# A four-layer hybrid trunk on one core: finer write tracking, head outputs copied out of PSUM, and a new order table

## The chip, the cores and the metric

The kernel runs on one core of one Trainium2 chip. Its time is device microseconds of one execution; three executions of the kernel before gave 1045.62, 1047.05 and 1047.22 us, a median of 1047.05 us. A profiled execution of the same kernel took 1047.38 us. The engines are named as in the profile: PE (TensorE, matrix products and transposes), DVE (VectorE), ACT (ScalarE), POOL (GpSimd), SP (which issues the DMA transfers here). PE writes to PSUM, the small accumulator memory; everything else lives in SBUF.

## The reference

The input is x, 512 tokens of 1024 channels, in float32. Four layers follow, and each adds its output to x. Layers 0 and 3 are differential attention (A), layer 1 is a Conformer convolution (B), layer 2 is latent attention (C). Each also makes a SiLU gate that multiplies its branch before the output projection. Cut to what the change touches:

```python
# A: 8 heads, two softmax maps a head, blocks of 128 queries, chunk-causal
wts = p[:, :, 0] - lam * p[:, :, 1]
outs.append(jnp.einsum('bhqk,bhkd->bhqd', wts, v[:, :, :e]))
o = _rms_norm(jnp.concatenate(outs, axis=2), sub_g) * (1.0 - lambda_init)
return (o * jax.nn.silu(gate)) @ w_out

# B: GLU, causal depthwise convolution of 31 taps, LayerNorm, SiLU, gate
u = a * jax.nn.sigmoid(b)
u = lax.conv_general_dilated(u, conv_w, padding=[(B_CONV - 1, 0)], ...) + conv_b
u = jax.nn.silu(_layer_norm(u, ln_g, ln_b))
return (u * jax.nn.silu(gate)) @ w_out
```

## The kernel before

The 1024 channels are 8 blocks of 128, the 512 tokens 4 tiles of 128. Every float32 product is made of three fast ones: each operand is split into a high half (a rounded copy, mostly a cast on ACT, L497) and a low half (the difference, L514 on DVE or L517 on POOL), and PE computes high·high, high·low and low·high (L460). A projection runs through weight pieces of 128×1024 (tiles such as `L_g_w`, `L_o_w`), which SP loads, ACT casts, and DVE or POOL completes. `Hh` and `Hl` are the two halves of the normalised input; `X` is the residual stream.

**Attention (layers 0 and 3).** For head h and query block j, PE makes two score tiles (`L_h5j_sc`), DVE takes the maximum, ACT the exponentials (`_p`), DVE combines the maps; PE transposes them (`_wtr`, L466), ACT copies that to SBUF (`_wt`, L497), and PE multiplies with V into the head's output `L_o` (four query blocks of 128 columns, one PSUM buffer of the tag `o`, of which there is one slot). Four Square instructions on ACT (`_osq`) with sums, a root on POOL (`_or_y`, L740) and `gate_o` on DVE (L526: output times root times gate G, written to V) finish the head; only then is the slot `o` free for the next head's products. G comes from gate chunk 1: ACT scales it, loads the SiLU table, applies SiLU to 128×2048 elements, and loads the exponential's table again. The tiles `L_ytr` are transposes of V for the output projection.

**Convolution (layer 1).** `L_u` holds the GLU's result. The 8 channel blocks are convolved in three ways: some on DVE by 30 multiply-adds (`L_c`, L526), some on POOL from products of ACT (`L_cq` += `L_ct`, L517; the last addition writes `L_cs`), and blocks 5, 6 and 7 on PE (`conv_phase`): the rows are moved by DMA to `L_u4x` buffers (four groups of 32 partitions), DVE makes banded weights `L_wa` (four for a block, through the two buffers of the tag `p`), and PE multiplies, 72 matmul records a block. Blocks of the first two kinds come back to token order by transposes (`L_ctr`), blocks of the third land so. The result is V; BN_STATS on DVE takes statistics, and once all 8 blocks are there, an aggregate, a root on POOL (`L_lnr_y`) and 8 TENSOR_SCALAR instructions (L535) normalise V. Then V is transposed (`L_ytr`), ACT applies SiLU (`L_yv`), DVE multiplies by the gate and splits into `L_y`, and the output projection `L_o` runs. Gate chunk 1 (`L_g_a`, 96 matmuls of 512 columns) has no part in the LayerNorm.

**What sets the order.** The program makes a list of nodes (one instruction, or a group that stays together). `Plan.order` (L571) gives every engine its fixed sequence: of the nodes whose inputs and buffer slots are ready, by a cost model, the one that can start first goes next, ties by priority. The priority is the place in the program plus a number from the table `SHIFT`, looked up by layer, tile and engine. Each engine then runs its sequence strictly in order and waits by semaphores. What a node depends on comes from `Buf` and `View` (L79 to L195): every buffer keeps its last writer and its readers for each grain of elements and each half of the 128 partitions (`halves`).

## Time and profile before

| | |
|---|---|
| median of 3 runs | 1047.05 us (1045.62 to 1047.22) |
| profiled execution, its own time | 1047.38 us |
| its span, first to last instruction | 1045.6 us |
| mean granted PE clock | 0.990 |
| PE busy | 1006.7 us |
| DVE busy | 762.4 us |
| ACT busy | 585.1 us |
| POOL busy | 194.8 us |

The span is what the trace covers; the 1.8 us between it and the execution's time lie outside. Names in the rows lose their numbers: `L_o` is any head's output or any output projection of any layer, `L_ytr` any of the transposes of V. `[5.04 <-DVE V L535]` behind a row says that its engine was idle for 5.04 us before it, and that what it waited for last was DVE's write of V at line 535. A row with x8 groups eight instructions that ran one after another.

### The profile page before, as it was taken

How to read it: one execution, taken by the hardware profiler on the slowest of the kernel's cores; microseconds unless marked ns; L12 is line 12 of the kernel's file. 1: busy time of each engine (PE TensorE's matmuls, PEld its weight loads, DVE VectorE, ACT ScalarE, POOL GpSimd, SP SyncE). 2: the span in 40 equal slices, each digit the busy share in tenths (PEclk: the TensorE clock that was granted, in tenths of full speed). 3: DMA queues.
4: the chain of work that ended last, by engine and by line, in shares of the span. 5: the costliest groups of instructions: out<-in, count | busy, mean ns of one | idle time of the engine just before them, and what ended most of it. 6: DMA issues, size and time to landing. Idle time of an engine off the chain costs nothing.

```text
span 1045.6 us, 15204 instructions
## 1 busy us (share of the span) xinstructions
PE 1006.7 (96%) x5204; PEld 846.2 (81%) x5204; DVE 762.4 (73%) x1970; ACT 585.1 (56%) x1222; POOL 194.8 (19%) x135
## 2 busy tenths in 40 slices
...
GB/s 235 93 101 122 61 122 121 66 87 56 41 61 121 122 89 101 66 90 1 73 83 78 71 50 61 22 39 101 119 72 152 38 84 121 102 81 120 22 21 81
DMA packets 74308, 87.53 MB, mean 84 GB/s; under 512 B 17109, under 2 KB 47701, under 8 KB 74232
## 3 DMA queue, kind: packets, MB, share of 16 engines
...
## 4 chain that ended last, share of the span: by engine, by line
PE 72%; DVE 14%; ACT 6%; issue 4%; POOL 2%; DMA 1%; SPq 0%; DVEq 0%; ACTq 0%; POOLq 0%
PE L_o L460 20%; PE L_g_a L460 14%; PE L_qk_a L460 12%; PE L_v_a L460 8%; DVE L_c L526 4%; PE L_ab_a L460 2%; PE L_c_a L460 1%; POOL L_cq L517 1%; PE L_c L460 1%; DVE L_qk_T L514 1%; PE L_qk_tr L466 1%; ACT G L490 1%; PE L_kv_a L460 1%; DVE L_qk_t L514 1%; PE L_h3j_sc L460 1%
## 5 line engine op out<-in xcount | busy, mean ns | idle before, releaser
L460 PE MATMUL L_qk_a<-L_qk_w,Hh 128*128 128x512 f32 x512 | 161.6, 397 | 0.0
L460 PE MATMUL L_o<-L_y,L_o_w 128*128 128x512 f32 x576 | 141.6, 395 | 0.0
L460 PE MATMUL L_g_a<-L_g_w,Hh 128*128 128x512 f32 x384 | 121.4, 397 | 2.3 <-ACT L_qk_sq L490 1.9
L460 PEld LDWEIGHTS L_o<-L_y,L_o_w 128*128 128x128 f32 x576 | 105.2, 188 | 21.1 <-POOL L_o_w L517 0.4
L740 POOL TENSOR_TENSOR L_h_or_y<-L_h_ov,minus_half 128x4 f32<-128x4 f32 x16 | 17.4, 1089 | 484.3 <-DVE L_h_ov L535 311.7
L460 PEld LDWEIGHTS L_qk_a<-L_qk_w,Hh 128*128 128x128 f32 x512 | 92.5, 188 | 16.8 <-ACT G L490 0.3
L460 PE MATMUL L_qk_a<-L_qk_w,Hl 128*128 128x512 f32 x256 | 100.5, 392 | 0.6 <-DVE Hl L526 0.6
L517 POOL TENSOR_TENSOR L_cq<-L_cq,L_ct 128x512 f32<-128x512 f32 x58 | 80.2, 1382 | 27.9 <-DMA L_ab_w_r<-b_w_in 21.3
L460 PE MATMUL L_ab_a<-Hh,L_ab_w 128*128 128x512 f32 x256 | 81.6, 393 | 3.0 <-DVE L_ab_sg L514 2.1
L460 PEld LDWEIGHTS L_g_a<-L_g_w,Hh 128*128 128x128 f32 x384 | 69.6, 188 | 16.6 <-ACT L_qk_sq L490 2.3
L460 PE MATMUL L_v_a<-L_v_w,Hh 128*128 128x512 f32 x256 | 81.0, 397 | 0.7 <-DVE L_qk_t L514 0.5
L460 PE MATMUL L_g_a<-L_g_w,Hl 128*128 128x512 f32 x192 | 75.2, 391 | 0.0
L526 DVE SCALAR_TENSOR_TENSOR L_c<-L_u,L_tab,L_c 128x512 f32<-128x512 f32 x90 | 65.0, 750 | 1.4
L490 ACT ACTIVATE L_ct<-L_u,L_tab 128x512 f32<-128x512 f32 x60 | 42.6, 721 | 33.3 <-POOL L_cq L517 31.6
L460 PEld LDWEIGHTS L_ab_a<-Hh,L_ab_w 128*128 128x128 f32 x256 | 47.9, 188 | 15.4 <-DVE L_ab_sg L514 2.0
L460 PEld LDWEIGHTS L_qk_a<-L_qk_w,Hl 128*128 128x128 f32 x256 | 48.0, 188 | 11.9 <-DVE Hl L526 1.7
L460 PEld LDWEIGHTS L_v_a<-L_v_w,Hh 128*128 128x128 f32 x256 | 46.2, 188 | 9.9 <-DVE L_qk_t L514 1.0
L517 POOL TENSOR_TENSOR L_sqs<-L_sqs,L_sq 128x512 f32<-128x512 f32 x21 | 32.1, 1528 | 98.3 <-ACT L_sq L490 84.5
L514 DVE TENSOR_TENSOR L_g_w<-L_g_w_r,L_g_w 128x1024 fp32r<-128x1024 f32 x32 | 43.9, 1374 | 8.8 <-ACT L_g_w L497 8.2
L460 PE MATMUL L_v_a<-L_v_w,Hl 128*128 128x512 f32 x128 | 50.1, 391 | 0.0
L460 PE MATMUL L_ab_a<-Hl,L_ab_w 128*128 128x512 f32 x128 | 49.9, 390 | 0.0
L497 ACT CAST L_o_w<-L_o_w_r 128x1024 fp32r<-128x1024 f32 x32 | 33.6, 1052 | 28.7 <-PE L_g_a L460 16.4
...
## 6 DMA issues: line engine op xcount, KB each, us to landing
...
```

The lines of the kernel that those rows point to most:

```text
L460: lambda nc: nc.tensor.matmul(out.real(), a.real(), b.real(), start=start, stop=stop),
L466: emit = lambda nc: nc.tensor.transpose(out.real(), src.real(), ident.real())
L490: nc.scalar.activation(out.real(), src.real(), func, scale=scale.real() if isinstance(scale, View) else scale, **kw)
L497: lambda nc: nc.scalar.copy(out.real(), src.real()), [src], [out])
L514: lambda nc: nc.vector.tensor_tensor(out=out.real(), in0=a.real(), in1=b.real(), op=op), [a, b], [out])
L517: lambda nc: nc.gpsimd.tensor_tensor(out=out.real(), in0=a.real(), in1=b.real(), op=op), [a, b], [out])
L526: self.add("dve", out.n / 960.0 + (0.13 if isinstance(scalar, View) else 0.068), lambda nc: nc.vector.scalar_tensor_tensor(out=out.real(), ...
L740: self.p.add("pool", 0.32 + 0.18 * v.n, lambda nc: nc.gpsimd.tensor_tensor(out=y.real(), in0=v.real(), in1=self.minus_half[:, 0:v.n].real( ...
```

## The change

Three things change. Lines below the edits move by 3 (L460 becomes L463, L497 becomes L500, L517 becomes L520).

First, the tracking of writes. Buffers of 544 elements a partition (the `u4` buffers of `conv_phase`) are tracked in grains of 8 elements, those of 1084 (the GLU's `u`) in grains of 2, where both had 32; and partitions in four parts of 32, where there were two halves of 64. An instruction depends on fewer others by that where it touches only a part of such a buffer.

Second, in layers 0 and 3 the outputs of heads 4, 5 and 6 are copied from the PSUM slot `o` to an SBUF buffer `oc`, one query block at a time, by ACT. The squares and the gate multiply read the copy. These are 24 more ACT instructions.

Third, the whole `SHIFT` table is replaced by other numbers. The program has the same instructions otherwise.

```diff
-        self.grain = 1 if size <= 64 else 6 if size == 192 else 32
+        self.grain = 1 if size <= 64 else 6 if size == 192 else 8 if size == 544 else 2 if size == 1084 else 32
...
-        self.writer = [None] * (2 * n)
-        self.readers = [[] for _ in range(2 * n)]
+        self.writer = [None] * (4 * n)
+        self.readers = [[] for _ in range(4 * n)]
...
-            v.halves = tuple(range((rows.start or 0) // 64, -(-(rows.stop or P) // 64)))
+            v.parts = tuple(range((rows.start or 0) // 32, -(-(rows.stop or P) // 32)))
...
 SHIFT = {k: int(v) for k, v in (x.split("=") for x in """
-L0_g0_a.act=5733 L0_g0_a.pe=-1495 L0_g0_w.dve=1051 L0_g0_w_r.sp=-99 L0_g1_a.act=4 L0_g1_a.pe=1821 L0_g1_w.act=-392
...
-        return 0.115 if len(out.halves) == 1 and out.n > 256 else 0.0
+        return 0.115 if len(out.parts) <= 2 and out.n > 256 else 0.0
...
             sq = self.buf("mid", N + "_osq")
+            if 4 <= h < 7:
+                own = self.buf("mid", N + "_oc", [P, NT, P])
+                for jb in range(NT):
+                    p.copy(own[:, jb, :], po[:, jb, :])
+                po = own
             for jb in range(NT):
                 p.act(sq[:, jb * P:(jb + 1) * P], po[:, jb, :], AF.Square, accum=ss[:, jb:jb + 1])
```

What the new table does to the order is seen in the engines' sequences. PE at the end of layer B, before (`L_g_a` are gate matmuls, `L_c` with `L_wa` is block 7, `L_ctr` the transposes of blocks 2, 4, 3 and, last, 1, `L_ytr` those of V):

```order
L460 MATMUL L_g_a_4296<-Hl,L_g_w_4280 128x512
L460 MATMUL L_g_a_4296<-Hh,L_g_w_4280 128x512
L466 MATMUL L_ctr_4519<-ident,L_cs_4084 128x128 x4
L466 MATMUL L_ctr_4527<-ident,L_cs_4329 128x128 x4
L466 MATMUL L_ctr_4549<-ident,L_cs_4532 128x128 x4
L460 MATMUL L_c_4379<-L_wa_0_4371,L_u_4380 128x128 x9
L460 MATMUL L_c_4379<-L_wa_1_4382,L_u_4380 128x128 x9
L460 MATMUL L_c_4379<-L_wa_2_4583,L_u_4380 128x128 x9
L460 MATMUL L_c_4379<-L_wa_3_4595,L_u_4380 128x128 x9
L466 MATMUL L_ctr_4606<-ident,L_cs_4035 128x128 x4
L466 MATMUL L_ytr_4639<-ident,V 128x128 x4
```

and with the change, from block 7 on (`L_ctr_4512` is block 3):

```order
L463 MATMUL L_c_4330<-L_wa_0_4358,L_u_4331 128x128 x9
L463 MATMUL L_c_4330<-L_wa_1_4371,L_u_4331 128x128 x9
L463 MATMUL L_g_a_4480<-Hh,L_g_w_4191 128x512
L463 MATMUL L_g_a_4480<-Hl,L_g_w_4191 128x512
L463 MATMUL L_g_a_4480<-Hh,L_g_w_4191 128x512
L463 MATMUL L_c_4330<-L_wa_2_4473,L_u_4331 128x128 x9
L463 MATMUL L_c_4330<-L_wa_3_4484,L_u_4331 128x128 x9
L469 MATMUL L_ctr_4512<-ident,L_cs_4499 128x128 x4
L463 MATMUL L_g_a_4520<-Hh,L_g_w_4191 128x512
```

Block 7 has moved into the gate chunk, and block 3 behind it. The end of a run of gate matmuls and the first three transposes of V, further down in the same sequence:

```order
L463 MATMUL L_g_a_4520<-Hl,L_g_w_4258 128x512
L463 MATMUL L_g_a_4520<-Hh,L_g_w_4258 128x512
L469 MATMUL L_ytr_4592<-ident,V 128x128 x4
L469 MATMUL L_ytr_4598<-ident,V 128x128 x4
L469 MATMUL L_ytr_4606<-ident,V 128x128 x4
L463 MATMUL L_g_a_4440<-Hh,L_g_w_4258 128x512
L463 MATMUL L_g_a_4440<-Hl,L_g_w_4258 128x512
```

Before, all 96 gate matmuls stood ahead of the transposes and of block 7. Now 24 of them do; between the last `L_ctr` and the first `L_ytr` stand 39, and the rest lie among and behind the first transposes of V, ahead of the output projection.

POOL at the same place (`L_cq` and `L_cs` are block 3's sums, `L_o_w` low halves of output weights, `L_lnr_y` the LayerNorm's root), before:

```order
L517 TENSOR_TENSOR L_cq_3616<-L_cq_3616,L_ct_27_4386 128x512
L517 TENSOR_TENSOR L_o_w_4397<-L_o_w_r,L_o_w_4397 128x1024
L517 TENSOR_TENSOR L_cq_3616<-L_cq_3616,L_ct_28_4409 128x512
L517 TENSOR_TENSOR L_cq_3616<-L_cq_3616,L_ct_29_4417 128x512
L517 TENSOR_TENSOR L_o_w_4454<-L_o_w_r,L_o_w_4454 128x1024
L517 TENSOR_TENSOR L_o_w_4484<-L_o_w_r,L_o_w_4484 128x1024
L517 TENSOR_TENSOR L_cs_4532<-L_cq_3616,L_ct_30_4459 128x128x4
L517 TENSOR_TENSOR L_o_w_4524<-L_o_w_r,L_o_w_4524 128x1024
L740 TENSOR_TENSOR L_lnr_y<-L_v,minus_half 128x4
```

and now:

```order
L520 TENSOR_TENSOR L_cq_3615<-L_cq_3615,L_ct_28_4471 128x512
L520 TENSOR_TENSOR L_cq_3615<-L_cq_3615,L_ct_29_4478 128x512
L520 TENSOR_TENSOR L_cs_4499<-L_cq_3615,L_ct_30_4496 128x128x4
L743 TENSOR_TENSOR L_lnr_y<-L_v,minus_half 128x4
L520 TENSOR_TENSOR L_o_w_4556<-L_o_w_r,L_o_w_4556 128x1024
L520 TENSOR_TENSOR L_o_w_4581<-L_o_w_r,L_o_w_4581 128x1024
L520 TENSOR_TENSOR L_o_w_4648<-L_o_w_r,L_o_w_4648 128x1024
L520 TENSOR_TENSOR L_o_w_4695<-L_o_w_r,L_o_w_4695 128x1024
```

The four low halves of the first column half have moved from among and behind block 3's sums to directly behind the root.

ACT in the tail of layer 3, with the change, around the SiLU of gate chunk 1 (`L_h_oc` is the copy of head 5's or 6's output, `L_y` the next layer's or the projection's operand). Before, the two table loads and the SiLU stood ahead of head 5's last exponentials; now they stand around head 6's second weight copy:

```order
L493 ACTIVATE L_h_osq,L_h_oss<-L_h_oc 128x128
L493 ACTIVATE L_y_9448<-L_ytr_9597,L_lay 128x512
L493 ACT_TABLE_LOAD
L493 ACTIVATE G<-G 128x4x512
L500 COPY L_h6j_wt<-L_h6j_wtr 128x256
L493 ACT_TABLE_LOAD
L493 ACTIVATE L_h6j_p,L_l_9533<-L_h6j_sc_9580,L_h6j_mx_9605,L_rq 128x384
L493 ACTIVATE L_h6j_p,L_l_9533<-L_h6j_sc_9585,L_h6j_mx_9619,L_rq 128x384
```

Head 5 and 6 have by then written their first blocks into `o`, since the copies freed it.

More of the change, by code (lines that the diff above doesn't have):

```diff
@@ L117, with __init__ @@
 class View:
-    def __init__(self, buf, ops, idx, halves=(0, 1)):
-        self.buf, self.ops, self.idx, self.halves = buf, ops, idx, halves
+    def __init__(self, buf, ops, idx, parts=(0, 1, 2, 3)):
+        self.buf, self.ops, self.idx, self.parts = buf, ops, idx, parts
     def _then(self, op, idx):
-        return View(self.buf, self.ops + [op], idx, self.halves)
+        return View(self.buf, self.ops + [op], idx, self.parts)
     def __getitem__(self, i):
@@ L192, in grains @@
             u = np.unique(self.idx // self.buf.grain)
-            g = self._g = np.concatenate([u + h * self.buf.n for h in self.halves])
+            g = self._g = np.concatenate([u + h * self.buf.n for h in self.parts])
         return g
@@ new lines @@
+L0_h5_mx.dve=-461 L0_h5_oc.dve=2810 L0_h5_or_y.dve=6 L0_h5_osq.act=-2916 L0_h5_oss.dve=-928 L0_h5_ov.dve=1999
+L0_h5_p.dve=-1658 L0_h5_sc.dve=79 L0_h5_sc.pe=3337 L0_h5_wtr.pe=-4014 L0_h6_cf.dve=-15978 L0_h6_mx.dve=-323
+L0_h6_oc.act=14 L0_h6_or_y.pool=706 L0_h6_ov.dve=-2033 L0_h6_p.act=541 L0_h6_p.dve=-17 L0_h6_sc.dve=-787
+L0_h6_wt.act=-1587 L0_h7_cf.dve=-3972 L0_h7_or_y.dve=-2174 L0_h7_osq.act=313 L0_h7_oss.dve=762 L0_h7_p.act=2782
+L0_h7_p.dve=72 L0_h7_sc.dve=1277 L0_h7_sc.pe=-40022 L0_h7_wt.act=-2131 L0_h7_wtr.pe=-101 L0_lay.act=-25
@@ new lines @@
+L0_lay.dve=2060 L0_lay.sp=-48 L0_o0.dve=-3000 L0_o0.pe=-367 L0_o00.dve=-464 L0_o00.pe=11813 L0_o01.dve=1011
+L0_o01.pe=799 L0_o02.pe=-118 L0_o03.dve=-6118 L0_o03.pe=3585 L0_o0_w.act=12126 L0_o0_w.dve=-6 L0_o0_w_r.sp=215
+L0_o1.dve=14987 L0_o1.pe=10205 L0_o10.dve=-793 L0_o10.pe=1537 L0_o11.pe=29 L0_o12.dve=-1188 L0_o12.pe=11357
+L0_o13.pe=24213 L0_o1_w.act=-789 L0_o1_w.dve=-12941 L0_o1_w_r.sp=5657 L0_o2.dve=-1022 L0_o2.pe=-472 L0_o3.dve=2
+L0_o3.pe=-2841 L0_o4.pe=966 L0_o5.pe=842 L0_o6.pe=5 L0_o7.pe=-1873 L0_qk0_T.dve=-2238 L0_qk0_a.pe=-99
@@ new lines @@
+L2_h1_sc.pe=-314 L2_h1_wtr.pe=-2815 L2_h2_mx.dve=1646 L2_h2_p.act=-278 L2_h2_sc.dve=1806 L2_h2_sc.pe=-2
+L2_h2_wt.act=3989 L2_h2_wtr.pe=1559 L2_h3_mx.dve=24439 L2_h3_p.act=-1349 L2_h3_sc.dve=6281 L2_h3_wt.act=-1133
+L2_h3_wtr.pe=2478 L2_h4_mx.dve=-599 L2_h4_p.act=4703 L2_h4_sc.dve=-1597 L2_h4_sc.pe=-19108 L2_h4_wt.act=2773
+L2_h4_wtr.pe=-1983 L2_h5_p.act=-2 L2_h5_sc.dve=-1611 L2_h5_wtr.pe=-8062 L2_h6_mx.dve=-1381 L2_h6_p.act=20833
+L2_h6_sc.dve=864 L2_h6_sc.pe=-5736 L2_h6_wtr.pe=-846 L2_h7_mx.dve=-65 L2_h7_p.act=-756 L2_h7_sc.dve=176
```

261 lines of the change are left out of this document (125 added, 136 removed).

## The prediction

> **What bounds the kernel now.** I read the page first: the shares of the engines and the chain that ended last.
>
> ```profile
> PE 1006.7 (96%) x5204; PEld 846.2 (81%) x5204; DVE 762.4 (73%) x1970; ACT 585.1 (56%) x1222; POOL 194.8 (19%) x135
> ...
> PE 72%; DVE 14%; ACT 6%; issue 4%; POOL 2%; DMA 1%; SPq 0%; DVEq 0%; ACTq 0%; POOLq 0%
> ```
>
> TensorE (PE) is the bound. The change leaves every matmul in place (3192 program rows on PE before and after), so it can win only what PE loses: 1045.6 − 1006.7 = 38.9 us of idle time, and what it runs at a lower clock. Busy time and granted clock by windows, cut at the places where PE idles most, say where that is (columns: span of the window, then PE, PEld, DVE, ACT, POOL busy, the clock, DMA share, GB/s):
>
> ```profile
> core 0: us, PE busy (x) PEld busy (x) DVE busy (x) ACT busy (x) POOL busy (x), PEclk, DMA share, GB/s
> 313.00:444.40 131.40, 127.73 (x635) 105.92 (x634) 124.05 (x179) 73.48 (x102) 98.29 (x67) 1.00 0.34 100
> 444.40:487.10 42.70, 34.61 (x191) 29.87 (x191) 24.49 (x64) 20.80 (x31) 16.54 (x10) 0.88 0.18 56
> 460.00:487.10 27.10, 19.01 (x123) 16.97 (x122) 21.64 (x56) 10.71 (x18) 4.60 (x3) 0.81 0.11 38
> 960.00:993.30 33.30, 27.02 (x153) 21.79 (x151) 24.41 (x80) 25.67 (x61) 2.02 (x2) 0.90 0.22 64
> 242.20:245.70 3.50, 3.49 (x17) 3.37 (x18) 0.75 (x1) 2.43 (x7) 0.00 (x0) 0.56 0.00 0
> ```
>
> The end of layer B's mixer (460.0 to 487.1) idles 27.10 − 19.01 = 8.1 us and its clock of 0.81 costs another 0.19 × 27.1 = 5.1 us: 13.2 us. The tail of layer 3's attention (960.0 to 993.3) idles 6.3 us and loses 0.10 × 33.3 = 3.3 us by the clock. Layer 0's tail has a spell at clock 0.56. The waits of PE, longest first (total, times, longest), name the releasers:
>
> ```profile
> PE L_ytr L466 <- DVE V L535: 5.0, 1, 5.0
> PE L_o L460 <- DVE V L526: 4.6, 2, 2.8
> PE L_ctr L466 <- ACT V L497: 2.1, 1, 2.1
> ```
>
> All three are the places that the new order touches. The timeline of PE through layer B's end (start, duration, operation, count, and the idle time before it):
>
> ```profile
> 459.86 0.39 PE L460 MATMUL L_g_a<-Hh,L_g_w 128*128 128x512 f32 x1
> 460.09 1.04 PE L466 MATMUL L_ctr<-ident,L_cs 128*128 128x128 f32 x8
> 463.19 0.63 PE L466 MATMUL L_ctr<-ident,L_cs 128*128 128x128 f32 x4 [2.06 <-ACT V L497]
> 463.65 9.83 PE L460 MATMUL L_c<-L_wa,L_u 128*128 128x128 f32 x72
> 473.32 0.60 PE L466 MATMUL L_ctr<-ident,L_cs 128*128 128x128 f32 x4
> 478.97 5.77 PE L466 MATMUL L_ytr<-ident,V 128*128 128x128 f32 x24 [5.04 <-DVE V L535]
> 485.19 0.66 PE L466 MATMUL L_ytr<-ident,V 128*128 128x128 f32 x4 [0.46 <-ACT L_yv L490]
> 486.38 0.66 PE L466 MATMUL L_ytr<-ident,V 128*128 128x128 f32 x4 [0.53 <-ACT L_yv L490]
> 486.80 3.46 PE L460 MATMUL L_o<-L_y,L_o_w 128*128 128x512 f32 x14
> ```
>
> The last gate matmul starts at 459.86 and the next operation 0.23 later: 0.23 us is the price of one 512-column matmul. After it PE has nothing but the LayerNorm's own chain. It waits 2.06 for channel block 3, convolves block 7 by matmul, transposes block 1, and waits 5.04 for the normalised V, with nothing else to run. 2.06 + 5.04 + 0.46 + 0.53 = 8.1 us, the idle time of that window.
>
> **The change, layer B's end.** The new order puts block 4, block 7 and block 3 ahead of 72 of the 96 matmuls of gate chunk 1 (blocks 2 and 1 earlier still), and the first four V transposes among the 72. Between the last block transpose and the first V transpose stand 39 matmuls: 39 × 0.23 = 9.0 us of PE work. What PE needs there, from 473.32 to 478.97, is 5.65 us, and its pieces on DVE are (ahead of them the row of the gate products)
>
> ```profile
> 458.25 2.74 DVE L514 TENSOR_TENSOR G<-L_g_a,L_tab 128x512 f32<-128x512 f32 x4 [12.75 <-PE L_g_a L460]
> ...
> 475.90 1.04 DVE L550 BATCH_NORM_AGGREGATE L_mv<-L_stat 128x2 f32<-128x48 f32 x4
> 476.97 0.17 DVE L535 TENSOR_SCALAR L_v<-L_mv 128x4 f32<-128x4 f32 x1
> 478.28 3.74 DVE L535 TENSOR_SCALAR V<-V,L_mv,L_lnr_y 128x512 f32<-128x512 f32 x8 [1.13 <-POOL L_lnr_y L740]
> ```
>
> So the 5.04 goes, with 3.3 us of cover to spare (9.0 − 5.65). The wait of 2.06 for block 3 goes too. Its last sum (L_cs) on POOL stood behind the low halves of output weights:
>
> ```profile
> 446.66 2.41 POOL L517 TENSOR_TENSOR L_o_w<-L_o_w_r,L_o_w 128x1024 fp32r<-128x1024 f32 x1
> 449.01 2.69 POOL L517 TENSOR_TENSOR L_cq<-L_cq,L_ct 128x512 f32<-128x512 f32 x2
> ...
> 460.84 1.28 POOL L517 TENSOR_TENSOR L_cs<-L_cq,L_ct 128x512 f32<-128x512 f32 x1 [2.47 <-PE L_ctr L466]
> 462.07 2.36 POOL L517 TENSOR_TENSOR L_o_w<-L_o_w_r,L_o_w 128x1024 fp32r<-128x1024 f32 x1
> ```
>
> Three of them are now behind it. Without the one at 446.66, POOL's additions end at 449.3 and L_cs at about 450.6 (449.01 + 2.69 − 2.41 + 1.28), an estimate from these rows, while PE comes to block 3 later than that: 72 gate matmuls (16.6 us) before 460, at 443.5, and then block 7's 8 us first. The 0.46 and 0.53 are short waits on ACT, and are covered by the gate matmuls too. With no idle time there, the half clock goes. Sum of what goes: 8.1 + 5.1 = 13.2 us.
>
> What comes instead, all on DVE, which was 124.05 of 131.40 us busy from 313.0 to 444.4 and has work moved forward onto it. (a) The second halves of blocks 6 and 7 wait for their weight products `wa`, which go through two buffers. In the new order DVE does three gate products (0.68 each, by the group below), a weight's low half (1.83, below) and block 6's sums and statistics (some 1.6 of the 2.6 us from 473.32 to 475.90, which held those of two blocks) between block 7's second and third `wa`: 5.5 us, and then 1.34 for that `wa`. In these 6.9 us PE has two quarters of block 7 (72 matmuls in 9.67 us, of which 1.7 is half clock: 2.0 a quarter) and three gate matmuls, 4.7 us: 2.2 us of idle time. At block 6 one `wa` comes late, 1.3. Bounds 0 and 6.9 + 1.3. (b) The last four V transposes wait for rows of V that now stand behind the four gate products (2.74 at 458.25): 2 us, bounds 0 and 2.8. Behind each wait all later gate or output matmuls queue, for PE runs in order. (a) and (b): 5.5 us, bounds 0 and 11.0. Layer B's end: −13.2 + 5.5 = **−7.7 us**.
>
> **POOL beside DVE.** The low halves of o_w, 2.4 us each, now follow the LayerNorm's root directly, beside V, y·gate and y on DVE. The trace shows what that can do (groups of DVE from 342.0 to 444.4, where POOL adds almost without pause; then one tile's minimum, median and maximum in 455 to 472):
>
> ```profile
> L514 DVE TENSOR_TENSOR L_g_w<-L_g_w_r,L_g_w 128x1024 fp32r<-128x1024 f32 x8 | 14.6, 1826 | 1.3 <-ACT L_g_w L497 1.0 <-POOL L_cq L517 0.3
> L514 DVE TENSOR_TENSOR L_wa<-L_d,wx 128x1152 f32<-128x1152 f32 x8 | 10.7, 1344 | 1.0 <-PE L_c L460 0.9
> ...
> L514 DVE TENSOR_TENSOR G<-L_g_a,L_tab 128x512 f32<-128x512 f32 x4 | 2.5, 676 | 0.0
> ...
> L514 DVE TENSOR_TENSOR L_tab<-L_setup x6: 267/280/2097, 462.6 to 468.8; 128x128 f32<-128x128 f32 x4, 128x256 f32<-128x256 f32 x2
> L514 DVE TENSOR_TENSOR L_g_w<-L_g_w_r,L_g_w x32: 1194/1225/2124, 51.8 to 946.7; 128x1024 fp32r<-128x1024 f32 x32
> ```
>
> A DVE operation with two SBUF inputs takes 1826 ns there against a median of 1225, and one of the two L_tab products took 2097 beside the POOL operation at 462.07. `wa`, with one input in PSUM, is not stretched (1344). I take 2 us of lateness at the V transposes beyond the others, hidden by the 3.3 us of cover: nothing on the path. [...]
>
> **The copies, layers 0 and 3.** Heads 4 to 6 free the one PSUM slot `o` after four ACT copies instead of after the gate multiply (L526). A copy of 128×128 from PSUM (the last row), behind the SiLU that the gate needs:
>
> ```profile
> 967.33 1.28 ACT L490 ACT_TABLE_LOAD   x1
> 968.62 1.91 ACT L490 ACTIVATE G<-G 128x2048 f32<-128x2048 f32 x1
> ...
> 980.31 0.26 ACT L497 COPY L_h6j_wt<-L_h6j_wtr 128x128 f32<-128x128 f32 x1
> ```
>
> and the two waits of PE for that multiply, in layers 0 and 3:
>
> ```profile
> 242.21 1.65 PE L460 MATMUL L_o<-V,L_h5j_wt 128*128 128x128 f32 x6 [1.74 <-DVE V L526]
> ...
> 971.74 1.65 PE L460 MATMUL L_o<-V,L_h5j_wt 128*128 128x128 f32 x6 [2.84 <-DVE V L526]
> ```
>
> 24 × 0.26 = 6.2 us more on ACT, which is 56% busy; the work that hides them is PE's, except at the tails, where ACT also holds the gate's SiLU between two table loads: 1.28 + 1.91 + 1.28 = 4.5 us. In the old order this stood ahead of head 4's gate multiply, which held `o` for head 5: the 2.84 and 1.74. Both go. In the new order the same 4.5 us stands ahead of head 6's second weight copy, for which PE has some 1.4 us of score and transpose work, so 4.5 + 0.4 − 1.4 = 3.5 us of idle time come in layer 3, and about 1.9 behind them, where the second table load delays the next exponentials. That is 5.4 us against 6.3 before: −0.9. In layer 0, 1.74 goes and two or three ACT waits of about a microsecond come: +0.4, bounds −3.4 (1.74 and the spell of 3.5 us at 0.56 gone) and +4.5 (the whole SiLU stretch on the path). I take **−0.5 us** for both, bounds −13 (all idle and slow time of both tails) and +5.
>
> The clock: in 242.20 to 245.70 it was 0.56, after 1.74 us of idle time that followed 2 us of transposes. [...]
>
> Finer tracking by itself issues nothing. It drops false dependencies, so that PE and DVE may start parts of a buffer earlier, which is in the orders counted above; elsewhere the rows are shifted by little.
>
> **Sum.** 1047.38 (profiled execution: span 1045.6 and 1.8 around it) − 7.7 − 0.5 = 1039.2. The median of the runs is 0.3 below that execution: **1038.9 us**, 1039 rounded.
>
> **Rivals.**
> First, *DVE is the bound of layer B's end*, the slower side. DVE had no idle time to give until 444. If the four `wa`, the gate's low half and the gate products that now come before the normalisation find it as full as before, PE stands at block 6, at block 7, at the V transposes and at y, each with 39 or fewer matmuls behind, and three half-clock spells. It decides when the new waits exceed 13.2 + 2: the 11.0 of (a) and (b), 6.3 at V (four POOL operations of 2.4 less 3.3 of cover) and 1.7 are 19.0, so 1047 + 5.8 − 0.5 = 1052.3. Against it: DVE sat idle for 12.75 us before 458.25, so it has room for what comes forward. Chance 0.12.
> [...] Chance 0.2.
> Third, *the tails win fully*: the copies take the waits and the slow spells out of layers 0 and 3: 1.74 + 1.7 + 6.3 + 3.3 = 13.0 less about 5 that stays: 1038.9 − 8 = 1030.9. Against it the table loads stay. Chance 0.13.
> Fourth, the change does not do what it says: the slot `o` is not what held head 5 and the wait moves elsewhere by the same size, with block 3 late as before: about 1047. Chance 0.05.
> The forecast: 0.5.
>
> **Range and chances.** The forecast's own range is 1035 to 1043 (terms (a) and (b) between 1.5 and 9.5). With the second and third rival the range is 1031.5 to 1047.2; what is left out is the first rival, the lower half of the third and half of the fourth, 0.2. No change that can be measured means within 0.2%, 2.1 us (1045.0 to 1049.1). Faster: 0.5 + 0.13 + 0.09 of the second = 0.72. Same: 0.09 of the second, 0.04 of the fourth, 0.03 of the first = 0.16. Slower: 0.12.
>
> **What would show it.** Right: no wait of `L_ytr` on V near 5 us, no wait of `L_ctr` of 2 us, clock 0.95 or more over the 40 us before layer B's output matmuls, and these some 7 us earlier against the program's start; PE waits on `wa` and on V of one to three microseconds in their place; L_o waits on V (L526) gone, and a wait of o on `wt` copies of about 3.5 us in layer 3. [...] Wrong altogether: PE's idle time in layer B's end as large as before, or the waits of DVE-fed products above 10 us.

## The result and the profile after

The changed kernel takes 1020.60 us (median; 1018.87 to 1021.28) against 1047.13 us for the kernel before (now the median of four executions): a ratio of 0.9746, 95% interval 0.9729 to 0.9763. The gain is 26.5 us, where 8 were forecast. The direction was right, the size was not, and the time lies below the range. The profiled execution took 1020.82 us, with a span of 1019.0 us and a mean granted clock of 0.998 (0.990 before).

The busy time on the page of the changed kernel:

```profile
PE 993.1 (97%) x5204; PEld 836.9 (82%) x5204; DVE 760.5 (75%) x1970; ACT 589.5 (58%) x1246; POOL 193.9 (19%) x135
```

PE's idle time fell from 38.9 to 25.9 us (1019.0 − 993.1), a gain of 13.0. The clock gives another 8.4: 0.010 of 1045.6 us was lost before, 0.002 of 1019.0 now. The 5.2 us left of the 26.6 in span lie in PE's busy time at full clock, in pieces too small to name; their cause stays open.

Where it lies shows when both programs are cut at the same amount of PE work. To cut them, the nominal durations of PE's instructions were added up in the order of each sequence, and both spans divided where the sums are equal. Then the difference of two windows is time won or lost in that stretch, whatever was moved inside it. The windows of the kernel before (length, then PE, PEld, DVE, ACT, POOL busy, clock, DMA share, GB/s):

```profile
0.00:287.60 287.60, 280.14 (x1436) 233.79 (x1437) 216.22 (x646) 173.37 (x393) 17.94 (x18) 0.99 0.35 100
287.60:404.10 116.50, 112.11 (x495) 90.25 (x494) 104.96 (x152) 62.12 (x89) 70.14 (x45) 1.00 0.35 100
404.10:454.20 50.10, 49.96 (x292) 43.42 (x290) 38.52 (x56) 31.76 (x43) 45.68 (x33) 1.00 0.25 75
454.20:497.20 43.00, 34.91 (x193) 30.13 (x192) 29.84 (x68) 18.06 (x28) 7.56 (x5) 0.88 0.12 39
497.20:578.60 81.40, 81.13 (x382) 68.79 (x380) 35.69 (x72) 32.79 (x69) 25.03 (x16) 1.00 0.27 77
578.60:689.80 111.20, 104.38 (x628) 90.39 (x627) 94.73 (x320) 79.25 (x198) 7.46 (x4) 1.00 0.19 56
689.80:943.10 253.30, 251.25 (x1288) 211.85 (x1287) 184.27 (x481) 136.55 (x289) 16.95 (x12) 1.00 0.30 90
943.10:1045.60 102.50, 92.83 (x504) 77.60 (x502) 58.16 (x179) 51.22 (x115) 4.03 (x4) 0.97 0.19 62
```

and of the changed kernel:

```profile
0.00:282.10 282.10, 275.23 (x1436) 229.72 (x1437) 215.91 (x648) 176.71 (x406) 17.60 (x18) 1.00 0.36 102
282.10:393.00 110.90, 110.53 (x513) 90.92 (x511) 100.98 (x148) 59.17 (x87) 65.85 (x42) 1.00 0.36 103
393.00:444.30 51.30, 49.82 (x316) 43.88 (x315) 45.42 (x76) 32.42 (x46) 46.72 (x34) 1.00 0.24 69
444.30:478.00 33.70, 30.97 (x150) 25.03 (x150) 28.74 (x51) 18.30 (x27) 12.40 (x5) 1.00 0.19 63
478.00:559.30 81.30, 80.95 (x382) 68.86 (x380) 34.60 (x73) 34.34 (x72) 24.41 (x16) 1.00 0.27 77
559.30:665.80 106.50, 102.89 (x624) 90.08 (x623) 91.49 (x312) 78.09 (x196) 6.54 (x4) 1.00 0.17 54
665.80:919.40 253.60, 251.53 (x1297) 211.84 (x1296) 187.06 (x508) 140.55 (x303) 17.35 (x13) 1.00 0.32 92
919.40:1019.00 99.60, 91.15 (x499) 76.55 (x497) 56.28 (x161) 49.87 (x116) 3.02 (x3) 0.98 0.20 64
```

The gain by stretch, the first length less the second, beside the forecast:

| stretch | gain, us | forecast |
|---|---|---|
| layer 0 (4.0 in its tail, 1.5 ahead of it) | 5.5 | −0.4 (tail), 0 ahead |
| layer 1, its start: the GLU's projections | 5.6 | 0 |
| layer 1, gate chunks and block 6 | −1.2 | |
| layer 1, its end: LayerNorm | 9.3 | 7.7 with the row above |
| seam of layers 1 and 2 | 0.1 | 0 |
| layer 2, its heads | 4.7 | 0 |
| layer 3 up to its tail | −0.3 | 0 |
| layer 3, its tail | 2.9 | 0.9 |
| sum | 26.6 | 8.2 |

The cuts hang on the nominal durations, most of all in layer 1, where the kinds of matmul changed places (495 records of PE before and 513 after in its first stretch, 193 and 150 in its last). Its three rows together, 13.7 us, are firmer than each of them. PE's idle time fell by 4.0 us at the start of layer 1 (4.4 to 0.4) and by 3.2 in layer 2 (6.8 to 3.6). Ahead of layer 0's tail it did not fall: in the first 225 us PE idles 5.4 us before and 6.8 after, so the 1.5 won there lies in its busy time.

The waits of PE in the changed kernel (total, times, longest) that stand in the place of the three shown before:

```profile
PE L_o L463 <- ACT L_h6j_wt L500: 2.5, 3, 1.8
PE L_h6j_wtr L469 <- DVE L_y L529: 2.4, 1, 2.4
PE L_ytr L469 <- DVE V L538: 1.6, 1, 1.6
...
PE L_c L463 <- DVE L_wa L517: 1.4, 2, 1.2
```

The 5.0 on V is 1.6, the 2.1 of `L_ctr` is gone, and so are the 4.6 us that `L_o` waited for V. The first two rows are layer 3's tail. PE's timeline at the end of layer 1:

```profile
439.56 4.29 PE L463 MATMUL L_c<-L_wa,L_u 128*128 128x128 f32 x36 [0.18 <-DVE L_wa L517]
...
453.02 0.49 PE L469 MATMUL L_ytr<-ident,V 128*128 128x128 f32 x3
455.15 1.20 PE L469 MATMUL L_ytr<-ident,V 128*128 128x128 f32 x9 [1.64 <-DVE V L538]
```

Block 7 costs no wait worth the name, and the transposes of V run into a wait behind the third of them, because DVE is slow there. DVE's timeline in the same place, and POOL's:

```profile
438.16 2.61 DVE L517 TENSOR_TENSOR L_wa<-L_d,wx 128x1152 f32<-128x1152 f32 x2
...
449.06 6.03 DVE L538 TENSOR_SCALAR V<-V,L_mv,L_lnr_y 128x512 f32<-128x512 f32 x4 [1.13 <-POOL L_lnr_y L743]
...
461.45 2.57 DVE L517 TENSOR_TENSOR L_y<-L_yv,L_y 128x512 fp32r<-128x512 f32 x1 [0.23 <-ACT L_y L500]
```

```profile
435.88 6.20 POOL L520 TENSOR_TENSOR L_cq<-L_cq,L_ct 128x512 f32<-128x512 f32 x4
...
449.00 2.40 POOL L520 TENSOR_TENSOR L_o_w<-L_o_w_r,L_o_w 128x1024 fp32r<-128x1024 f32 x1
452.30 2.51 POOL L520 TENSOR_TENSOR L_o_w<-L_o_w_r,L_o_w 128x1024 fp32r<-128x1024 f32 x1 [0.90 <-ACT L_o_w L500]
```

Four normalising operations take 6.03 us where eight took 3.74 before. They begin just as POOL's low halves do. Taken one by one, the first and the last of the four are held:

```profile
449.06 2.62 DVE L538 TENSOR_SCALAR V<-V,L_mv,L_lnr_y 128x512 f32<-128x512 f32 x1 [1.13 <-POOL L_lnr_y L743]
...
452.52 2.58 DVE L538 TENSOR_SCALAR V<-V,L_mv,L_lnr_y 128x512 f32<-128x512 f32 x1
```

Each of these ends about 0.3 us after the POOL operation beside it (451.40 and 454.81). The two between them, from 451.60 on, take 0.99 us together.

### The profile page after: what moved, and what is told of

Its sections match the earlier page's. It is cut to its first block, busy times and chain, and to the rows that moved or that the text cites. A ratio compares the mean times of both kernels' runs of the same rounds, so it can differ in the third digit from the quotient of the medians.

```text
span 1019.0 us, 15165 instructions
## 1 busy us (share of the span) xinstructions
PE 993.1 (97%) x5204; PEld 836.9 (82%) x5204; DVE 760.5 (75%) x1970; ACT 589.5 (58%) x1246; POOL 193.9 (19%) x135
## 4 chain that ended last, share of the span: by engine, by line
PE 77%; DVE 9%; POOL 5%; ACT 4%; issue 2%; DMA 2%; SPq 0%; ACTq 0%; DVEq 0%; POOLq 0%
PE L_o L463 21%; PE L_qk_a L463 16%; PE L_g_a L463 13%; PE L_v_a L463 8%; PE L_ab_a L463 4%; POOL L_cq L520 4%; DVE L_c L529 2%; PE L_qk_tr L469 1%; PE L_c_a L463 1%; DMA L_qk_st<-L_qk_st 1%; DMA L_x<-x 1%; PE L_ytr L469 1%; PE L_h4j_sc L463 1%; PE L_h7j_sc L463 1%; PE L_h5j_sc L463 1%
## 5 line engine op out<-in xcount | busy, mean ns | idle before, releaser
L463 PE MATMUL L_qk_a<-L_qk_w,Hh 128*128 128x512 f32 x512 | 161.9, 397 | 0.0
L463 PE MATMUL L_o<-L_y,L_o_w 128*128 128x512 f32 x576 | 141.6, 396 | 1.1 <-DVE L_y L517 0.6
L463 PEld LDWEIGHTS L_o<-L_y,L_o_w 128*128 128x128 f32 x576 | 105.3, 188 | 22.4 <-DVE L_y L517 1.0
L463 PE MATMUL L_g_a<-L_g_w,Hh 128*128 128x512 f32 x384 | 121.1, 396 | 1.6 <-ACT L_qk_sq L493 1.6
L743 POOL TENSOR_TENSOR L_h_or_y<-L_h_ov,minus_half 128x4 f32<-128x4 f32 x16 | 17.2, 1077 | 467.2 <-DVE L_h_ov L538 149.9
L463 PEld LDWEIGHTS L_qk_a<-L_qk_w,Hh 128*128 128x128 f32 x512 | 92.3, 188 | 16.4 <-DVE X L517 0.2
L463 PE MATMUL L_qk_a<-L_qk_w,Hl 128*128 128x512 f32 x256 | 100.3, 392 | 0.0
L520 POOL TENSOR_TENSOR L_cq<-L_cq,L_ct 128x512 f32<-128x512 f32 x58 | 80.2, 1384 | 30.4 <-ACT L_ct L493 26.8
L463 PEld LDWEIGHTS L_g_a<-L_g_w,Hh 128*128 128x128 f32 x384 | 69.5, 188 | 15.2 <-ACT L_qk_sq L493 2.1
L463 PE MATMUL L_v_a<-L_v_w,Hh 128*128 128x512 f32 x256 | 81.1, 398 | 0.0
L463 PE MATMUL L_ab_a<-Hh,L_ab_w 128*128 128x512 f32 x256 | 80.7, 392 | 0.4 <-DVE L_ab_sg L517 0.4
L463 PE MATMUL L_g_a<-L_g_w,Hl 128*128 128x512 f32 x192 | 75.1, 391 | 0.0
L517 DVE TENSOR_TENSOR L_qk_w<-L_qk_w_r,L_qk_w 128x1024 fp32r<-128x1024 f32 (+1 forms) x30 | 35.3, 1186 | 30.5 <-ACT L_qk_w L500 30.4
L493 ACT ACTIVATE L_ct<-L_u,L_tab 128x512 f32<-128x512 f32 x60 | 42.7, 721 | 25.9 <-POOL L_cq L520 25.0
L463 PEld LDWEIGHTS L_ab_a<-Hh,L_ab_w 128*128 128x128 f32 x256 | 48.0, 188 | 11.3 <-issue 0.8
L463 PEld LDWEIGHTS L_qk_a<-L_qk_w,Hl 128*128 128x128 f32 x256 | 48.0, 188 | 10.8 <-DVE Hl L529 0.3
L500 ACT CAST L_qk_st<-L_qk_tr 64x512 fp32r<-64x512 f32 x64 | 37.2, 581 | 29.3 <-PE L_qk_tr L469 28.0
L463 PEld LDWEIGHTS L_v_a<-L_v_w,Hh 128*128 128x128 f32 x256 | 45.8, 188 | 8.4 <-DVE L_qk_t L517 0.3
L517 DVE TENSOR_TENSOR L_g_w<-L_g_w_r,L_g_w 128x1024 fp32r<-128x1024 f32 x32 | 43.8, 1374 | 9.9 <-ACT L_g_w L500 9.3
L463 PE MATMUL L_v_a<-L_v_w,Hl 128*128 128x512 f32 x128 | 50.1, 392 | 0.0
L463 PE MATMUL L_ab_a<-Hl,L_ab_w 128*128 128x512 f32 x128 | 49.9, 390 | 0.0
```

The costliest lines, as they stand in the source:

```text
L463: lambda nc: nc.tensor.matmul(out.real(), a.real(), b.real(), start=start, stop=stop),
L493: nc.scalar.activation(out.real(), src.real(), func, scale=scale.real() if isinstance(scale, View) else scale, **kw)
L500: lambda nc: nc.scalar.copy(out.real(), src.real()), [src], [out])
L517: lambda nc: nc.vector.tensor_tensor(out=out.real(), in0=a.real(), in1=b.real(), op=op), [a, b], [out])
L520: lambda nc: nc.gpsimd.tensor_tensor(out=out.real(), in0=a.real(), in1=b.real(), op=op), [a, b], [out])
L743: self.p.add("pool", 0.32 + 0.18 * v.n, lambda nc: nc.gpsimd.tensor_tensor(out=y.real(), in0=v.real(), in1=self.minus_half[:, 0:v.n].real( ...
```

## The experiments

All times are medians; "+" is against the changed kernel's 1020.6 us, ratios are to the kernel before with their 95% intervals.

### One part at a time, planned anew

The change has three parts, so the first four kernels leave one out or keep one alone, and let the planner make the order again.

```diff
# e1: the changed code with the old table;  e2: the old code with the new table
# e3: no copies
-            if 4 <= h < 7:
+            if False:
# e4: old tracking
-        self.grain = 1 if size <= 64 else 6 if size == 192 else 8 if size == 544 else 2 if size == 1084 else 32
+        self.grain = 1 if size <= 64 else 6 if size == 192 else 32
-            v.parts = tuple(range((rows.start or 0) // 32, -(-(rows.stop or P) // 32)))
+            v.parts = tuple(range((rows.start or 0) // 64, -(-(rows.stop or P) // 64)))
```

> The changed kernel (finer tracking and the copies of heads 4 to 6) with the old table of numbers. Theory O (the gain is the new order alone, and the other two edits do little without it): 1045 to 1055 us, since the old numbers were not made for this list of nodes. Theory S (the copies and the finer tracking carry most of it, whatever the numbers): at most 1034 us, half of the 26.5 gained.

> The kernel before with nothing but the new table of numbers: no copies, old tracking. Theory O: 1020 to 1028 us. Theory S: over 1034 us.

> The changed kernel without the copies of heads 4 to 6; new numbers, finer tracking. By the accounting of the two traces the tails of layers 0 and 3 gained 4.0 and 2.9 us. Theory O: the copies are worth less than these 7, so 1021 to 1027. Theory S: the tails' 7 us come back and more, since the numbers count on the freed slot: 1028 to 1035.

> The changed kernel with the old tracking (grains of 32, two halves); new numbers, copies. Theory O: within 2 us of 1020.6, the tracking only lets the planner see a few parts earlier. Theory S: blocks 5 to 7 of layer B come later and their early place is lost: 1024 to 1032.

| kernel | us | ratio to before |
|---|---|---|
| e1, old table | 1090.82 | 1.0428 (1.0392 to 1.0464) |
| e2, new table alone | 1082.45 | 1.0331 (1.0309 to 1.0354) |
| e3, no copies | 1061.47 | 1.0134 (1.0112 to 1.0157) |
| e4, old tracking | 1044.63 | 0.9984 (0.9967 to 1.0001) |

Both code edits under the old table are 44 us slower than before; the new table under the old code is 35 us slower. Only the three together are clearly faster. Neither theory's range holds e1, e3 or e4, and e2 is over theory S's 1034 but slower than both kernels. Waits of PE in e2 show what kind of loss this is:

```profile
PE L_g_a L463 <- DVE L_qk_T L517: 7.9, 1, 7.9
PE L_o L463 <- DVE V L529: 6.1, 1, 6.1
PE L_c L463 <- DMA L_u<-L_u: 6.0, 1, 6.0
```

The first and the third stand in neither kernel, and the second is twice the longest of its kind before (2.8). The numbers shift priorities in a sequence that is built step by step, so they fit one list of nodes with one set of dependences; any other list makes another sequence with the same numbers, and waits at places that neither kernel had. So these four runs can't say which part carries the gain. The same holds by layer. In four more kernels the old numbers stand for the keys of one layer:

```diff
+SHIFT = {k: v for k, v in SHIFT.items() if not k.startswith("L0_")} | OLD_L0   # e5; e6, e7, e8: L1_, L2_, L3_
```

> The changed kernel with the old numbers for layer 0 alone. If the gain is laid down layer by layer and adds up, the accounting of the two traces by the matmul work done (5.5 us gained by the end of layer 0) says 1026 us. If the copies take layer 0's gain whatever the numbers: 1020.6.

> The old numbers for layer 1 alone. Adding up: 13.7 us gained in layer 1 (4.4 before gate chunk 1, 9.3 at the LayerNorm), so 1034 us. Against that: if the end of layer 1 is set by what the layer before leaves, less than half of it, 1027 or lower.

> The old numbers for layer 2 alone. Adding up: 4.7 us, 1025 us. If layer 2's waits went because layer 1 ended in another state (buffers and loads earlier) and not by its own numbers: 1020.6.

> The old numbers for layer 3 alone, with the copies. Adding up: 2.7 us, 1023 us. If the copies alone free head 5 there: 1020.6 or less.

Layer 0: 1053.77 (+33.2), layer 1: 1040.11 (+19.5), layer 2: 1051.73 (+31.1), layer 3: 1034.54 (+13.9). If the parts added up, 1026, 1034, 1025 and 1023 were expected. The sum is 98 us, for a change that brought 26.5. These runs say that the numbers hang together, and nothing on shares.

### The sequence held fixed

From here on the planner's choice is replaced by a list of ranks: of the nodes that can go, the one with the lowest rank goes next. With the changed kernel's own sequence as ranks, one thing at a time can be moved without a new plan for the rest. The ranks fix the sequence only as long as every node can go in its turn: where a buffer slot is not free, a later rank goes first. That matters for e14 to e16, where slots are taken back.

```diff
-                for n in c:
-                    ...
-                    key = (max(est2, f + 0.02), n.prio)
-                    ...
+                for n in cand[e]:
+                    if best is None or RANK[n.seq] < best[0]:
+                        st = slot_time(n)
+                        if st is not None:
+                            best = (RANK[n.seq], n, max(free[e], n.ready, st))
```

**The LayerNorm's cover (e9).** The ranks put PE's products of block 7 and the transposes of block 3 behind the last matmul of gate chunk 1, as in the old kernel, with what depends on them.

> The changed kernel in its own order, one thing moved: on PE block 7's convolution and block 3's transposes go behind the last matmul of gate chunk 1, with what hangs on them; every other instruction keeps its place. If the gain at the LayerNorm is the cover by gate matmuls: at least the 9.3 us come back that the two traces differ by there, and up to 14, since V's normalisation, 6.03 us beside POOL in this order, then lies open too: 1030 to 1035 us, with a wait of the V transposes on V of over 5 us and a lower clock. If the cover was not what won: under 1024.

1030.53 us, ratio 0.9856 (0.9830 to 0.9881): +9.9. PE's timeline there:

```profile
452.41 8.20 PE L671 MATMUL L_c<-L_wa,L_u 128*128 128x128 f32 x72
...
466.09 4.31 PE L677 MATMUL L_ytr<-ident,V 128*128 128x128 f32 x16 [5.04 <-DVE V L746]
474.20 4.08 PE L671 MATMUL L_o<-L_y,L_o_w 128*128 128x512 f32 x8 [3.80 <-ACT L_y L708]
```

The wait of 5.04 is back to the hundredth, and the 16 transposes behind it take 4.31 us, 0.27 each, against 0.13 in the changed kernel (1.20 for 9, at a clock of 1.00) and 0.24 in the kernel before (5.77 for 24, at 0.54). By these times the half clock is back with it; the mean granted clock of that execution is 0.987, against 0.998. The wait of 3.80 on `L_y` stood in neither kernel: the 33 gate matmuls that stand between the transposes of V and `L_o` in the changed kernel had to go ahead of the transposes too. So e9 shows that the cover by gate matmuls is what won, and prices it only to between 6 us (9.9 less 3.8) and 10; the windows say 8.1 (9.3 less 1.2).

**Finer tracking (e10).** The changed kernel's own sequence with the old tracking. Seven memsets of padding move on DVE and two small loads change places, nothing else.

> The changed kernel with the old tracking of writes, held to the changed kernel's own order: PE, ACT and POOL have the same sequences, DVE writes seven pads of zeros in other places, two small loads are swapped. Theory O (tracking is bookkeeping of the planner and nothing on the chip waits for it): 1020.6, give or take 2. Theory S (the moves of blocks 5 to 7 wait for each other under the old tracking): 15 to 20 us for each block, over 1060.

1020.78 us, ratio 0.9756 (0.9732 to 0.9779): no difference from the changed kernel. Beside e4's 1044.63 this says what the tracking does. It costs and wins nothing on the chip; it takes dependences out of the planner's view that the chip never paid for in this sequence, and without it the planner does not find the sequence.

**POOL beside DVE (e11).** Four low halves of output weights go to DVE, behind the four operations on V; two of them are those of the POOL rows above.

```diff
-            p.tt(w[:, 1, ks, 0:cols], raw[:, ks, 0:cols], w[:, 0, ks, 0:cols].f32(), ALU.subtract, self.lo_eng)
+            p.tt(w[:, 1, ks, 0:cols], raw[:, ks, 0:cols], w[:, 0, ks, 0:cols].f32(), ALU.subtract,
+                 "dve" if name.startswith("L1_o0_w") else self.lo_eng)
```

> The changed kernel in its own order, with the four low halves of the first output weights of layer 1 on DVE instead of POOL, behind the rows of V that PE waits for first. If POOL's operations hold DVE's: V's first four rows take 1.9 us again instead of 6.03, the waits on V (1.6) and y (0.6) go, and 1.5 to 3 us are gained: 1017.6 to 1019.1, although DVE has 4 x 1.22 = 4.9 us more to do. If they do not: 0 to 3 us slower, 1020.6 to 1023.6.

1019.07 us, ratio 0.9733 (0.9710 to 0.9757). DVE:

```profile
449.82 1.92 DVE L746 TENSOR_SCALAR V<-V,L_mv,L_lnr_y 128x512 f32<-128x512 f32 x4 [1.13 <-POOL L_lnr_y L933]
```

and PE:

```profile
453.75 1.47 PE L677 MATMUL L_ytr<-ident,V 128*128 128x128 f32 x12
```

The four operations take 1.92 us instead of 6.03, and PE's wait for V is gone; `L_o` waits 0.86 us for G instead of 0.45. The time is 1.5 us shorter, but the two intervals overlap, so e11 can't be told from the changed kernel. What the trace settles is the cause: the stretch by 4.1 us is POOL's doing, and 1.6 of it reached PE. In the changed kernel the two held operations, 2.62 and 2.58 us instead of some 0.5, lost 4.1 us together, and each ended just after the POOL operation beside it (2.40 and 2.51). How POOL's operations hold DVE's no run shows.

**The start of layer 1 (e12).** In the first 60 us of PE work of layer 1 the nodes of all engines, some 260, stand in the old relative order; the rest is held.

> The changed kernel in its own order, but the instructions of a stretch of 60 us at the start of layer 1 (some 260, on all engines) stand in the order that the kernel before gave them. If the small waits there (before: 1.02, 1.52, 0.85 on DVE; after: 0.53) went by the order of that stretch alone: 3 to 6 us come back, 1024 to 1027. If they went because layer 0's tail leaves DVE less behind: under 1022.

1027.05 us, ratio 0.9820 (0.9793 to 0.9846): +6.5. The waits of PE that come back:

```profile
PE L_ab_a L671 <- DVE L_ab_sg L725: 2.0, 2, 1.4
...
PE L_ab_a L671 <- DVE L_ab_w L725: 1.2, 1, 1.2
...
PE L_ab_a L671 <- DVE Hl L737: 0.9, 1, 0.9
```

In the kernel before, the first two were 2.1 and 0.9; the third stood in neither kernel. PE was held there by the GLU's sigmoid product and by low halves of weights, both on DVE, which had 104.96 of 116.50 us to do in that stretch. The new order gives them to PE in time.

**Layer 2 (e13).** The same for the first 100 us of PE work of layer 2.

> The changed kernel with its sequence held fixed, except that the instructions of all engines in the first 100 us of PE work of layer 2 stand in the old relative order. Theory (layer 2's part of the gain comes from its own new order, for all engines are moved there by the new numbers): PE's lost time in that stretch was 2 to 5 us smaller after the change, so the time is 1022.7 to 1026, and the small waits of layer 2 that went (score matmuls and weight transposes of head pairs on copies and statistics, 0.7 to 1.7 us each) are back. Rival (layer 2 gains only because layer 1 hands it DVE with less work left over): below 1021.7, no wait returns.

1031.22 us, ratio 0.9855 (0.9825 to 0.9886): +10.6, more than the theory's 2 to 5.4. Its profiled execution, the shortest of them, has +7.7 in span (1026.7). The theory holds in kind and the rival (nothing lost) falls; PE's timeline has the old waits, 1.07 and 1.74 in the kernel before, again:

```profile
619.74 0.50 PE L671 MATMUL L_h2j_sc<-L_p_st 128*128 128x256 f32 x2 [1.08 <-DVE L_p_st L725]
...
623.70 0.89 PE L677 MATMUL L_h2j_wtr<-ident,L_h2j_p 128*128 128x128 f32 x3 [1.75 <-ACT L_h2j_p L701]
626.90 1.65 PE L671 MATMUL L_kv_a<-L_kv_w,L_lat 128*128 128x512 f32 x3 [1.07 <-ACT V L708]
```

Its third wait stood in neither kernel (0.45 on another producer before). So undoing a stretch costs more than the stretch had brought: the seams with the rest add losses of their own.

### What the copies are worth

**No copies, the same ranks (e14).**

> The changed kernel without the 24 copies, every other instruction in the changed kernel's sequence. Theory (the copies are worth what the two tails gained, 4.0 us in layer 0 and 2.9 us in layer 3): 1027 to 1029. Rival (the new sequence leans on the free slot: PE's products of heads 5, 6 and 7 stand so early that without the copies they wait for the gate multiply behind the SiLU, and everything queued behind them waits too): the waits of L_o on V come back at 5 us or more each in both attention layers, 1035 or more. Second rival (the copies are worth nothing, only the new numbers are): within 2 us of 1020.6.

1052.77 us, ratio 1.0063 (1.0041 to 1.0084): +32.2, and slower than the kernel before. The theory (the two tails' 7 us) falls, the first rival stands. Layer 1's first matmul starts at 314.6 us against 292.9 in the changed kernel, 21.7 us later; the distance stays so up to the start of layer 3, and layer 3 adds the rest, some 11. Windows over both tails of e14:

```profile
225.00:314.60 89.60, 77.54 (x381) 63.00 (x380) 50.20 (x140) 50.49 (x109) 4.71 (x5) 0.90 0.17 50
946.00:1012.00 66.00, 55.51 (x301) 46.03 (x300) 44.97 (x137) 38.37 (x92) 2.60 (x3) 0.90 0.19 57
```

In layer 0's: 89.60 − 77.54 = 12.1 us idle, and 0.10 × 89.6 = 9.0 us of lost clock. The changed kernel has next to nothing of either there:

```profile
224.00:292.90 68.90, 68.85 (x374) 57.69 (x373) 50.79 (x141) 49.90 (x109) 4.70 (x5) 1.00 0.22 66
```

PE's timeline in e14 says why: first what stands behind layer 0's gate chunk, then head 5 in layer 3:

```profile
239.59 7.02 PE L670 MATMUL L_o<-L_y,L_o_w 128*128 128x512 f32 x30
246.58 0.49 PE L670 MATMUL L_o<-V,L_h5j_wt 128*128 128x128 f32 x2
...
256.62 0.80 PE L670 MATMUL L_h6j_sc<-L_qk_st 128*128 128x256 f32 x2 [4.01 <-ACT L_h6j_p L700]
...
972.76 1.65 PE L670 MATMUL L_o<-V,L_h5j_wt 128*128 128x128 f32 x6 [6.38 <-DVE V L736]
```

And in the changed kernel:

```profile
230.09 1.06 PE L463 MATMUL L_o<-V,L_h5j_wt 128*128 128x128 f32 x8
...
944.26 0.83 PE L463 MATMUL L_o<-V,L_h5j_wt 128*128 128x128 f32 x6
```

Without a copy, head 4's output sits in the slot `o` until the gate multiply, and that needs the whole of gate chunk 1 and its SiLU. So head 5's products stand behind all gate matmuls, in layer 0 behind 30 output matmuls too, and in layer 3 wait 6.38 us; then heads 5 to 7 are left with too little other work to hide their exponentials, and PE waits 4.01 for them. With a copy head 5 runs inside the gate chunk (at 230.09 and 944.26, gate matmuls before and behind), and head 6 among gate and output matmuls. The copies don't just remove a wait of 1.7 and 2.8 us. They make two chains independent, and PE fills the one with the other. The ranks are those of the changed kernel, but a product whose slot is held is passed over, so PE's sequence in both tails is not the changed kernel's. The 32.2 us are therefore what an order made for the freed slot loses without it, and not what the copies brought.

**A whole layer as it was (e15, e16).** No copies in layer 0 (e15) or layer 3 (e16), and that layer's instructions in the old relative order, as far as the slots allow.

```diff
-            if 4 <= h < 7:
+            if 4 <= h < 7 and not N.startswith(("L0",)):     # e16: "L3"
```

> The changed kernel with all of layer 0 as it was: no copies there, and its instructions on every engine in the old relative order; layers 1 to 3 in the new sequence, held fixed. Theory (layer 0's new design is worth what the comparison of the two traces puts into it): 5.5 us, so 1025 to 1027, and layer 1 starts 5 to 7 us later than in the changed kernel. Rival (the new layer 1 is fitted to what the new layer 0 leaves behind, weights loaded early and DVE's backlog, so that an old layer 0 costs more than the old kernel lost in it): 1032 or more, with new waits of PE in the first 60 us of layer 1.

> The same for layer 3: no copies there, its instructions in the old relative order, layers 0 to 2 in the new sequence, held fixed. Theory (worth of the new tail by the comparison of the two traces): 2.9 us, so 1023 to 1025. Rival (at the seam between layers 2 and 3 the old order wants weights and statistics earlier than the new layer 2 leaves them): 1029 or more. Without copies but in the new sequence layer 3 had cost 10.9 us more; an old order that costs less shows that the old sequence was the better one for a kernel without copies, by the difference.

e16: 1025.65 us (1023.15 to 1027.21), ratio 0.9809 (0.9780 to 0.9839), +5.0: just above the theory's 1023 to 1025 and below the rival's 1029. So layer 3's copies and new order together are worth some 5 us by this run and 2.9 by the windows; its runs spread over 4 us. Without copies the old order of layer 3 is better than the new one by about 6 us (11 less 5): it was made for a slot that is held. e15: 1038.51 us, ratio 0.9927 (0.9903 to 0.9950), +17.9, where the theory expected 5.5 and the rival 12 or more. Layer 1's first matmul comes at 307.1, 14.2 us later than in the changed kernel and 8 later than in the kernel before. So most of the 17.2 us of span (1036.2 less 1019.0) is lost in layer 0 itself, and some 3 behind it, which is all that the rival's reason can hold. PE waits in both at places where neither kernel waits more than 0.3 us:

```profile
30.17 0.50 PE L670 MATMUL L_qk_a<-L_qk_w,Hl 128*128 128x512 f32 x1 [1.92 <-DVE Hl L736]
...
319.48 0.50 PE L670 MATMUL L_ab_a<-Hl,L_ab_w 128*128 128x512 f32 x1 [1.32 <-DVE Hl L736]
```

The old layer 0 isn't reproduced either: in the first 35 us PE, DVE and ACT do parts of their work in another order than in the kernel before. So e15 doesn't price layer 0's own share. The windows say 5.5 us; which part of that is the copies' and which the order's stays open.

## Why the prediction was wrong in size

**Layer B's end, −7.7: right.** The windows give 9.3 won at the LayerNorm and 1.2 lost just ahead of it, 8.1 in all; e9 costs 9.9. The 13.2 us that were to go went, with the half clock. Of the 5.5 us of new waits, (a) was 1.4 for 3.5 (1.2 at an earlier block, 0.2 at block 7, where 2.2 were expected) and (b) 1.6 for 2.0. With smaller waits that had no term PE idled 4.2 us in the two stretches (1.5 and 2.7), and about 1 us more came in its busy time, so it is partly luck that the sum comes within half a microsecond. But (b) came from another cause: the first group of transposes waits, not the last, and for V's operations, two of which POOL held (2.62 and 2.58 us), not for the gate products. The cover of 39 gate matmuls was there as worked out. The wait for block 3 went, but its reading was wrong: by the rows shown there, `L_cs` waited 2.47 us for PE's earlier transposes, when the low halves had ended at 458.37, and PE's 2.06 ended with ACT's copy of V.

**POOL beside DVE, 0 on the path: right within 1.6.** POOL's operations did hold DVE's. But no run shows the 6.3 us (four POOL operations of 2.4 less 3.3 of cover) that the first rival counts at V and that the range above 1043 leaves room for. The four did not lie end to end on the way from V to y: two fell beside V, a third beside one `L_y` (2.57 instead of 0.69). Most of the 4.1 us at V was lost in cover, and 1.6 reached PE.

**The tails, −0.5: mis-sized, 6.9 measured.** In layer 3 the term counted idle time alone, 5.4 us for 6.3. Idle time fell from 9.7 to 8.5 in that stretch, about as forecast. The other 1.7 is about what the clock gave, which the term left at nothing: the half-clock spell lasted 6.8 us before (968.9 to 975.7, clock 0.50) and 3.5 now (954.2 to 957.7, 0.51). Of the waits that came, only the second is the one that was named, behind the SiLU, with 1.81 us for 3.5:

```profile
951.49 0.44 PE L469 MATMUL L_h6j_wtr<-ident,L_h6j_p 128*128 128x128 f32 x2 [2.44 <-DVE L_y L529]
953.74 0.76 PE L463 MATMUL L_o<-V,L_h6j_wt 128*128 128x128 f32 x4 [1.81 <-ACT L_h6j_wt L500]
```

The first is DVE's: `L_y` reads `L_ytr`, which has the same PSUM tag as `_wtr`, and stood behind a low half of 1.22 us. In layer 0 the forecast was +0.4, and 4.0 were won: the wait of 1.74 and its spell at 0.56 went, which the term had only as its bound of −3.4, and the ACT waits of 2.1 us in sum that it put against them did not come at all, which fits that head 5 now runs inside the gate chunk. What failed is that the term left the clock out in both layers and, in layer 0, put in waits that no row showed. The third rival, "the tails win fully", was the nearest: its layer 0 part came true, and its layer 3 part partly. (Its 1030.9 still holds the −0.5 that it replaces; 1031.4 was meant.) e14 adds that the new order of both tails leans on the freed slot: 21.7 and 11 us are lost when it is taken back.

The miss is 18.4 us of span (26.6 less 8.2): 0.4 at layer B's end, 6.4 in the tails, 11.6 elsewhere.

**The step that failed** most is the sentence behind the terms: "elsewhere the rows are shifted by little", taken as 0. Elsewhere 11.6 us were won: 1.5 in layer 0 ahead of its tail, 5.6 at the start of layer 1, 4.7 in layer 2, and −0.2 in the rest. Of the 38.9 us that PE idled, the three places hold 8.1, 6.3 and 1.7; the other 22.8 were given no term and, worse, no bound, though a new table moves rows everywhere. The waits were in the profile that was read (2.1 and 0.9 on the GLU's products, 1.7 and 1.1 in layer 2), each too small to be looked at alone. e12 and e13 show that they hang on the order in their own stretch. They are only half of it: PE's idle time elsewhere fell by some 5.8 us (4.0 and 3.2, less the 1.4 that came ahead of layer 0's tail), and the other half of the 11.6 lies in PE's busy time, with no cause shown. A bound from "all small waits stay" to "half of them go" would have put the lower end of the range at about 1020 (1031.5 less 11.4), though the half is a guess made afterwards.

**Finer tracking, 0: right on the chip** (e10), with the reason given turned round: it does not let the engines start earlier, it lets the planner see that they may.

**The clock.** At layer B's end the forecast was 0.95 or more; it is 1.00. One half-clock spell is left, in layer 3's tail, behind waits of 2.44 and 1.81 us:

```profile
955.80:957.00 1.20, 1.19 (x3) 0.85 (x4) 1.06 (x4) 1.17 (x6) 0.00 (x0) 0.50 0.00 0
```

The wait of 1.64 at V left the clock alone (1.00 from 455.1 to 458.6), where 1.74 in layer 0 had brought a spell before (0.56 from 242.2 to 245.7). Behind the 5.04 of the kernel before it was 0.54 (478.97 to 484.7). What decides between 1.64 and 1.74 stays open. The 1.7 us that the first and the third rival count for a spell is half of layer 0's 3.5 us, an estimate: the row there gives 0.44 × 3.5 = 1.5. No run shows a new wait at that price in layer B; the spell left in layer 3 costs 0.49 × 3.5 = 1.7.
